# RWKV-7 recurrence: alpha and key-times-a kept in DRAM between two stages, and the head normalisation on ScalarE

## The chip, the cores and the metric

One NeuronCore of one Trainium2 chip runs the whole program. The metric is device time in microseconds, from the start to the end of one execution. A NeuronCore has a matrix engine (PE, with weight loads listed as PEld), VectorE (DVE), ScalarE (ACT), GpSimd (POOL) and SyncE (SP). In this kernel SP issues every DMA, in the order of its queue.

## The reference

The program is one inference step of a two-layer decoder trunk on 1040 prompt tokens (16 of them learned) and 8 x 8 sample tokens: a gated DeltaNet layer, then an RWKV-7 layer. The change is in the second. Cut to it:

```python
r, k, v, z = rkvz
a     = sigmoid(a0 + (xs[5] @ a1) @ a2)
kk    = l2norm((k * k_k).reshape(B, T, H, N))          # 16 heads of 64
k     = k * (1.0 + (a - 1.0) * k_a)
decay = exp(-exp(w))
b     = kk * a
def step(S, (r_t, k_t, v_t, d_t, kk_t, b_t)):
    S = S * d_t + (S @ -kk_t) (x) b_t + v_t (x) k_t
    return S, S @ r_t
y = (y - mean(y)) * rsqrt(var(y) + GN_EPS) * lnx_w + lnx_b      # per head
y = (y + sum(r * k * r_k) * v) * silu(z)
out = y @ w_o
```

## The kernel before, in words

The 1104 tokens are cut into three segments of 384, 384 and 336 columns and every segment into six chunks of 64; two heads share the 128 partitions, so there are 8 pairs of heads and 24 items (segment, pair). The recurrence is computed chunk by chunk. With D the running product of decays in a chunk, the kernel forms `alpha = kk * D` (shifted by one token), `kk * a / D`, `r * D` and `k2 / D`, and a triangular system per chunk links them.

Two stages of the RWKV layer matter here.

The **inverse stage** (`rwkv_inverse`, five batches of up to five items) runs beside the big projections. For each item it loads the running decays, `a` and `k` (`rwkv_load`), computes `kk`, `D` (`Dp`) and its inverse (`iD`) on ScalarE (`rwkv_keys`), alpha into the tile `al` (a single buffer, name `sal` in the profile) on VectorE with small fixes on GpSimd (`alpha`), and `kk * a * iD` in place in `kk` (GpSimd, then VectorE). Matmuls of `kk` against `al` give the triangular matrices, which go through DRAM (`rltd`) to be inverted; the inverses are stored to DRAM (`ttd`).

The **recurrence** (`wave`) goes through 58 waves. In a wave up to three items are each at one of their chunks; an item is in work for six waves, and a new one is begun every second wave. `rwkv_front` prepares an item: it loads the same three inputs and `r` and `v` again, computes `kk`, `Dp` and `iD` again, and builds two operands. `AR` holds alpha and `r * D`; alpha is made by GpSimd (L1280, L1281, L1283), `r * D` by VectorE (L1354). `BK` holds `k2 * iD` (VectorE, L1357 and L1361) and `kk * a * iD` (GpSimd, L1358 and L1362). Then `pr` (L1367) is made for the bonus term. Later waves take the item's parts: `scores` (matmuls of `BK` against `AR` into the PSUM tiles `fG`, masked by VectorE into `G`, L1391 and L1393), `keys` (transposes of `BK` into `fBT`, copied by ScalarE into `BT`, L1402), `values` (transposes of `v` into `fVT`, copied by ScalarE into the ring `UV`, L1415) and `bonus`. All these PSUM tiles share a ring of two buffers with the name `f`.

The chain of a wave is: `step_solve` (PE, then ScalarE's copy into `X`, L1483), `step_inner` (PE, then two ScalarE evictions into `UV`, L62), `step_state` (PE `rS` and `rY`, then VectorE's update of the state, L1525, which needs ScalarE's `pre`, and ScalarE's copy of the outputs into `y`, L1533). Between these, PE works on the output projection and the gate projection; their weights come as tiles `wraw`, split into a high half `whi` (ScalarE, L86) and a low half `wlo` (GpSimd, L90).

`rwkv_finish` normalises an item's outputs over each head. VectorE takes mean and variance (`bnst`, `mv`), GpSimd a power (`grs`, L103) which VectorE refines (L104 to L106), and GpSimd applies them chunk by chunk, six operations of 128 x 64 (L1551). In the next but one wave PE transposes `y` (`fyT`). The sample states of the first eight items are read (`rwkv_sample_read`, with matmuls against `AR`) and written (`rwkv_sample_write`) in the first 16 waves or so.

PE's instructions in the recurrence stand in the order in which the program gives them. The order on all other engines, SP's DMAs among them, and PE's outside the recurrence, is set by a scheduler that simulates the program while it is built.

Of the kernel before, what the change touches and what calls it, by code (L numbers as in the profile page):

```python
# [10 lines left out]
AF = mybir.ActivationFunctionType  # L11
ALU = mybir.AluOpType
# [23 lines left out]
class Builder:  # L36
# [8 lines left out]
    def t(self, pool, shape, tag, bufs=1, dt=F32):  # L45
        self.uid += 1
        return pool.tile(shape, dt, name=f"{tag}_{self.uid}", tag=tag, bufs=bufs)
# [1200 lines left out]
    def rwkv_open(self):  # L1248
        self.rk2 = self.t(self.cp, [128, 144], "rk2")
        self.csd, self.ad, self.rd, self.vd, self.zd, self.kd = (self.dram([8, 128, 1152], n) for n in  # L1250
                                                                 ("csd", "ad", "rd", "vd", "zd", "kd"))
        self.ttd = self.dram([24, 128, 384], "ttd")

    def rwkv_load(self, n, pool, tag, names):
        nc, t = self.nc, self.t
# [9 lines left out]
    def rwkv_keys(self, p, ld, pool, tag):  # L1265

        nc, t = self.nc, self.t
        kk = t(pool, [128, 384], tag + "kk", 2 if tag == "s" else 1)
        self.act(kk, ld["k"], AF.Identity, scale=self.pcol["rwkv_k_k"][:, p:p + 1])
        Dp, iD = t(pool, [128, 385], tag + "Dp", 1), t(pool, [128, 384], tag + "iD", 1)  # L1270
        nc.gpsimd.memset(Dp[:, 0:1], 1.0)
        self.act(Dp[:, 1:385], ld["cs"], AF.Exp, scale=-self.DEC)
        self.act(iD, ld["cs"], AF.Exp, scale=self.DEC)
        return kk, Dp, iD

    def alpha(self, al, kk, Dp, s, eng):

# [10 lines left out]
    def rwkv_inverse(self, b, pool):  # L1288

        items = range(5 * b, min(5 * b + 5, 24))  # L1290
        nth = 6 * len(items)
        nc, t = self.nc, self.t
        ltd, ssd = self.dram([nth, 128, 64], f"rltd{b}"), self.dram([nth, 128], f"rssd{b}")
        for q, n in enumerate(items):
            s, p = divmod(n, 8)
            names = ("cs", "a", "k")
            ld = self.ahead or self.rwkv_load(n, pool, "s", names)
            kk, Dp, iD = self.rwkv_keys(p, ld, pool, "s")

            self.ahead = self.rwkv_load(n + 1, pool, "s", names) if n < 23 else None  # L1300
            sq = t(pool, [128, 384], "sgl", 2)
            self.act(sq, kk, AF.Square)
            al = t(pool, [128, 6, 64], "sal", 1)
            self.alpha(al, kk, Dp, s, nc.vector)
            nc.gpsimd.tensor_tensor(kk, kk, ld["a"], op=ALU.mult)
            nc.vector.tensor_tensor(kk, kk, iD, op=ALU.mult)
            gp = self.ps("f", 2, "L")
            ssp = self.ps("f", 2, "rss")
            for c in range(6):
                for h in (0, 1):  # L1310
                    a = 64 * h
                    self.mm(gp[a:a + 64, 64 * c:64 * c + 64], kk[a:a + 64, 64 * c:64 * c + 64], al[a:a + 64, c, :])
            self.mm(ssp[0:2, 0:384], self.hmask, sq)
            gl = t(pool, [128, 6, 64], "sgl", 2)
            nc.scalar.copy(gl, gp[:, 0:384].rearrange("p (c i) -> p c i", i=64))
            if s == 0:
                nc.gpsimd.tensor_tensor(gl[:, 0, :], gl[:, 0, :], self.m_strs2, op=ALU.mult)
            nc.sync.dma_start(ltd[6 * q:6 * q + 6].rearrange("c q i -> q c i"), gl)
# [12 lines left out]


    def rwkv_front(self, p, s):

        nc, t, ap, fp, col = self.nc, self.t, self.ap, self.fp, self.pcol
        P = Ctx()
        P.p, P.s, P.n = p, s, 8 * s + p
        NB = self.NB
# [4 lines left out]
        def system():  # L1343
            nc.sync.dma_start(P.TT.rearrange("p c k -> p (c k)"), self.ttd[P.n])
        ld = self.rwkv_load(P.n, fp, "f", ("cs", "k", "a", "r", "v"))
        kk, Dp, iD = self.rwkv_keys(p, ld, fp, "f")
        DC = P.DC = t(fp, [128, 14], "DC", NB + 2)
        nc.gpsimd.tensor_copy(DC[:, 0:6].unsqueeze(2), Dp[:, 1:385].rearrange("p (c k) -> p c k", k=64)[:, :, 63:64])
        if s == 0:
            nc.gpsimd.tensor_copy(DC[:, 6:14].unsqueeze(2), Dp[:, 1:65].rearrange("p (c k) -> p c k", k=8)[:, :, 7:8])  # L1350
        AR = P.AR = t(fp, [128, 6, 2, 64], "AR", NB + 1)
        c6 = lambda x: x.rearrange("p (c k) -> p c k", k=64)
        self.alpha(AR[:, :, 0, :], kk, Dp, s, nc.gpsimd)
        nc.vector.tensor_tensor(AR[:, :, 1, :], c6(ld["r"]), c6(Dp[:, 1:385]), op=ALU.mult)  # L1354
        k2 = t(fp, [128, 384], "k2", 1)
        self.act(k2, ld["a"], AF.Identity, scale=pc("rwkv_k_a"), bias=self.omka[:, p:p + 1])
        nc.vector.tensor_tensor(k2, k2, ld["k"], op=ALU.mult)  # L1357
        nc.gpsimd.tensor_tensor(kk, kk, ld["a"], op=ALU.mult)  # L1358

        BK = t(fp, [128, 6, 2, 64], "BK", 2)  # L1360
        nc.vector.tensor_tensor(BK[:, :, 0, :], c6(k2), c6(iD), op=ALU.mult)  # L1361
        nc.gpsimd.tensor_tensor(BK[:, :, 1, :], c6(kk), c6(iD), op=ALU.mult)  # L1362
        flat = lambda x: x.rearrange("p x k -> p (x k)")
        yield P

# [14 lines left out]
        def scores(c):  # L1380

            gp = [self.ps("f", 2, "G") for h in (0, 1)]
            for u in range(3):
                for h in (0, 1):
                    q = slice(64 * h, 64 * h + 64)
                    self.mm(gp[h][:, 128 * u:128 * u + 128], flat(BK[q, c + u]), flat(AR[q, c + u]))
            for h in (0, 1):
                g3 = gp[h][:, 0:384].rearrange("p (q k) -> p q k", k=128)
                f = 0
                if s == 0 and c == 0:  # L1390
                    nc.vector.tensor_tensor(G[:, 0, h, :], g3[:, 0, :], self.gms, op=ALU.mult)  # L1391
                    f = 1
                nc.vector.tensor_tensor(G[:, c + f:c + 3, h, :], g3[:, f:3], self.gm.unsqueeze(1).broadcast_to([128, 3 - f, 128]),  # L1393
                                        op=ALU.mult)
# [67 lines left out]
    def step_solve(self, W):  # L1462

        hs = [slice(0, 64), slice(64, 128)]
        UV = self.ring_uv(W.tau)
        for (P, ci), q in zip(W.items, W.at):
            for h in (0, 1):
                self.mmw(W, "X", h, 64 * q, P.G[:, ci, h, 0:64], UV[:, q, h])
        for (P, ci), q in zip(W.items, W.at):
            if 6 * P.s + ci > 1:  # L1470
                S = self.S[P.p]
                for x, name in ((0, "X"), (1, "Y")):
                    for h in (0, 1):
                        self.mmw(W, name, (h + x) % 2, 64 * q, P.AR[hs[h], ci, x], S[hs[h]])
        nc = self.nc
        lo, hi = min(W.at), max(W.at) + 1
        P, ci = W.items[-1]
        with self.tc.high_priority():
            if P.s == 0 and ci == 0:
                hi -= 1  # L1480
                nc.vector.tensor_tensor(W.X[:, hi], W.pX[:, 64 * hi:64 * hi + 64], P.xs[:, 0], op=ALU.add)
            if lo < hi:
                nc.scalar.copy(W.X[:, lo:hi].rearrange("p c k -> p (c k)"), W.pX[:, 64 * lo:64 * hi])  # L1483
# [51 lines left out]
    def rwkv_finish(self, p, s, P):  # L1535

        nc, t, ap, col = self.nc, self.t, self.ap, self.pcol
        c0, n = SEGS[s]
        y = lambda q: self.ring_y(2 * P.n + q)[:, 2 - q // 2]
# [7 lines left out]
        va, rs = t(ap, [128, 6], "va", 2), t(ap, [128, 6], "grs", 2)  # L1547
        nc.vector.tensor_scalar(va, mv[:, :, 1], GN_EPS, None, op0=ALU.add)
        self.rsqrt(rs, va, ap, "gn")
        for q in range(6):  # L1550
            nc.gpsimd.tensor_scalar(y(q), y(q), mv[:, q, 0:1], rs[:, q:q + 1], op0=ALU.subtract, op1=ALU.mult)  # L1551
        yield
        yp = self.ps("f", 2, "yT")
        for q in range(6):
# [17 lines left out]
    def rwkv_sample_read(self, P):  # L1572
# [16 lines left out]
        for b in range(8):  # L1589
            for h in (0, 1):  # L1590
                a = 64 * h
                self.mm(rp[a:a + 64, 16 * b:16 * b + 16], P.Sb[a:a + 64, b, :], AR[a:a + 64, 0, :, 8 * b:8 * b + 8])
        q = t(ap, [128, 2, 8, 8], "rkst", 1)
        nc.vector.tensor_copy(q, rp[:, 0:128].rearrange("p (b x r) -> p x b r", b=8, x=2))
        yield
# [373 lines left out]
```

## Time and profile before

| | us |
|---|---|
| median of 3 runs | 2374.34 |
| lowest and highest | 2370.59, 2375.54 |
| the profiled execution's own time | 2374.91 |
| its span | 2373.2 |
| inverse stage beside the projections | about 1465 to 1845 |
| recurrence | about 1845 to the end |

| engine | busy us | share of the span |
|---|---|---|
| PE | 2168.7 | 91% |
| VectorE | 1617.0 | 68% |
| ScalarE | 1248.0 | 53% |
| GpSimd | 1113.8 | 47% |

A row of the profile gives line, engine, operation, and what is written and read by the program's names; `[2.04 <-DVE G L1393]` at the end of a row of the timeline says that the engine stood idle for 2.04 us before it until VectorE's `G` of line 1393 was done. An SP row is the issue of a DMA, not its transfer. Shares are means over stages that have different limits.

### The profile page before, as it was taken

To read this page: it belongs to the slowest core of one execution; us is meant where nothing else is said; L and a number is where in the kernel's file an instruction comes from. 1 tells how busy PE (TensorE), PEld (TensorE's weight loads), DVE (VectorE), ACT (ScalarE), POOL (GpSimd) and SP (SyncE) were. 2 spreads that over 40 slices of the span, in tenths; PEclk is the share of its full clock that TensorE was granted. 3 is DMA by queue.
4 is the path that set the end of the run, shared out by engine and by line. 5 is a ranking of instruction groups with operands and counts; after the bars stand their busy time and mean duration, and the time that the engine had idled before them with its cause. 6 is when DMAs were issued, how large, how long until landed. Compare 5 with 4: busy or idle time off the path is not lost. (4 is left out here: it accounts for less than half of the span.)

```text
span 2373.2 us, 54463 instructions
## 1 busy us (share of the span) xinstructions
PE 2168.7 (91%) x19737; PEld 1962.9 (83%) x19737; DVE 1617.0 (68%) x4195; ACT 1248.0 (53%) x3479; POOL 1113.8 (47%) x1566
## 2 busy tenths in 40 slices
PE   5989999999999999999989998998999888888886
PEld 5888989888898989898989998987878776777775
DVE  6868677685858686873346724389896666778754
ACT  5455655554656555566243646555453454556552
POOL 3435343343444353433223513355454666777764
PEclk9999999999999999999999999999999999999998
DMA  3323332324233333435262245566754544555543
GB/s 113 106 74 104 87 102 78 96 71 113 68 105 94 85 98 88 115 107 163 62 165 76 72 156 173 143 164 165 188 135 129 178 115 141 158 178 182 178 138 125
DMA packets 470535, 290.01 MB, mean 122 GB/s; under 512 B 188121, under 2 KB 455642, under 8 KB 470266
## 3 DMA queue, kind: packets, MB, share of 16 engines
q1 hardware_dynamic: 470266, 286.53, 42.7%
q8 instruction: 156, 2.56, 0.5%
q14 instruction: 113, 0.93, 0.1%
HBM read 200.53 MB, written 85.89 MB: 121 GB/s over the span
## 5 line engine op out<-in xcount | busy, mean ns | idle before, releaser
L90 POOL TENSOR_TENSOR wlo<-wraw,whi 128x512 fp32r<-128x512 f32 (+2 forms) x252 | 329.7, 1311 | 349.2 <-ACT whi L86 323.2
L76 PE MATMUL d<-xc,whi 128*128 128x384 f32 (+2 forms) x910 | 259.1, 341 | 4.8 <-POOL xc L90 2.8
L86 ACT CAST whi<-wraw 128x512 fp32r<-128x512 f32 (+2 forms) x252 | 151.6, 603 | 130.6 <-PE dq L76 50.5
L419 DVE SCALAR_TENSOR_TENSOR cvy<-raw,cw,cvy 128x408 f32<-128x408 f32 (+2 forms) x288 | 178.9, 634 | 17.6 <-ACT cvy L62 15.7
L452 DVE TENSOR_TENSOR invtmp<-invA,invT 72x31 f32<-72x31 f32 (+31 forms) x403 | 170.4, 423 | 13.0 <-DMA invA<-ltd 5.1
L76 PEld LDWEIGHTS d<-xc,whi 128*128 128x128 f32 (+1 forms) x910 | 167.8, 191 | 12.6 <-issue 5.3
L454 DVE TENSOR_TENSOR invT<-invT,invtmp 72x31 f32<-72x31 f32 (+31 forms) x403 | 168.9, 419 | 6.7
L76 PE MATMUL dz<-xc,whi 128*128 128x384 f32 (+1 forms) x480 | 148.3, 340 | 0.0
L76 PE MATMUL dv<-xc,whi 128*128 128x384 f32 (+1 forms) x480 | 146.8, 335 | 0.0
L76 PE MATMUL d<-xc,wlo 128*128 128x384 f32 (+2 forms) x428 | 142.7, 342 | 0.0
L76 PE MATMUL d<-xa,whi 128*128 128x384 f32 (+3 forms) x450 | 139.0, 344 | 3.3 <-DVE xa L90 1.7
L868 POOL TENSOR_SCALAR Sb<-Sb,eglb 128x128 f32<-128x128 f32 x128 | 81.3, 651 | 88.1 <-DMA Sb<-in_state_gdn 23.7
L1551 POOL TENSOR_SCALAR y<-y,mv,grs 128x64 f32<-128x64 f32 x144 | 83.8, 599 | 42.8 <-DVE grs L106 40.0
L76 PE MATMUL dv<-xa,whi 128*128 128x384 f32 (+1 forms) x288 | 99.9, 347 | 0.1
L76 PE MATMUL dz<-xa,whi 128*128 128x384 f32 (+1 forms) x288 | 99.5, 346 | 0.0
L76 PEld LDWEIGHTS d<-xa,whi 128*128 128x128 f32 (+1 forms) x450 | 84.3, 192 | 9.7 <-issue 3.3
L76 PEld LDWEIGHTS dz<-xc,whi 128*128 128x128 f32 x480 | 88.9, 191 | 0.8
L76 PEld LDWEIGHTS dv<-xc,whi 128*128 128x128 f32 x480 | 88.5, 188 | 0.5 <-issue 0.4
L76 PE MATMUL d<-xh,wlo 128*128 128x384 f32 (+1 forms) x256 | 85.2, 348 | 1.6 <-POOL wlo L90 1.6
L76 PE MATMUL d<-xa,wlo 128*128 128x384 f32 (+3 forms) x252 | 86.4, 343 | 0.0
L76 PE MATMUL d<-xh,whi 128*128 128x384 f32 (+1 forms) x256 | 84.5, 344 | 0.5 <-ACT whi L86 0.5
L76 PE MATMUL d<-xl,whi 128*128 128x384 f32 (+1 forms) x256 | 84.5, 347 | 0.0
(514 smaller groups left out, 7171.7 us busy)
## 6 DMA issues: line engine op xcount, KB each, us to landing
wraw<-in_gdn_w_in SPq DMA_DIRECT2D x96, 256.0 KB
wraw<-in_rwkv_w_rkvz SPq DMA_DIRECT2D x80, 256.0 KB
Sb<-in_state_gdn SPq DMA_DIRECT2D x64, 256.0 KB
wraw<-in_rwkv_w_o SPq DMA_DIRECT2D x40, 256.0 KB
E<-drow SPq DMA_DIRECT2D x24, 384.0 KB
attn<-drow SPq DMA_DIRECT2D x24, 384.0 KB
wraw<-in_gdn_w_out SPq DMA_DIRECT2D x36, 256.0 KB
out_s_gdn<-Sb SPq DMA_DIRECT2D x32, 256.0 KB
```

Source lines behind the costliest of these rows:

```text
L76: self.nc.tensor.matmul(out, lhsT, rhs, start=start, stop=stop)
L86: nc.scalar.copy(hi, x)
L90: e.tensor_tensor(lo, x, hi.bitcast(F32), op=ALU.subtract)
L419: nc.vector.scalar_tensor_tensor(y[:, 0:wd], raw[:, k:k + wd], cw[k], y[:, 0:wd], op0=ALU.mult, op1=ALU.add)
L452: nc.vector.tensor_tensor(tmp, A[:, j, j + 1:32].unsqueeze(2).broadcast_to([nb, n, m]), Tv[:, j, 0:m].unsqueeze(1).broadcast_to([nb, n, m] ...
L454: nc.vector.tensor_tensor(Tv[:, j + 1:32, 0:m], Tv[:, j + 1:32, 0:m], tmp, op=ALU.subtract)
L868: nc.gpsimd.tensor_scalar(Sb[:, u], Sb[:, u], self.eglb[:, hv, 4 * g + u:4 * g + u + 1], None, op0=ALU.mult)
L1551: nc.gpsimd.tensor_scalar(y(q), y(q), mv[:, q, 0:1], rs[:, q:q + 1], op0=ALU.subtract, op1=ALU.mult)
```

## The change

Three things are done.

1. The inverse stage stores `al` and `kk * a * iD` of each item to two new DRAM arrays (`ald`, `bkd`): 48 DMAs of 192 KB.
2. The front of the recurrence no longer computes `kk`, alpha and `kk * a * iD`. It loads them: 24 DMAs into `AR` and 24 into every second block of 64 columns of `BK`. `AR` changes its layout from `[6, 2, 64]` to `[2, 6, 64]`, and its readers follow. `rwkv_keys` is split, so that the front calls only the decay part.
3. `y` is normalised on ScalarE as `rs * y + nm`, where `nm = -mean * rs` (tile `gnm`) is one more small VectorE operation, instead of `(y - mean) * rs` on GpSimd.

```diff
-        self.ttd = self.dram([24, 128, 384], "ttd")
+        self.ttd, self.ald, self.bkd = (self.dram([24, 128, 384], n) for n in ("ttd", "ald", "bkd"))
...
     def rwkv_keys(self, p, ld, pool, tag):
-        kk = t(pool, [128, 384], tag + "kk", 2 if tag == "s" else 1)
+        kk = t(pool, [128, 384], tag + "kk", 2)
         self.act(kk, ld["k"], AF.Identity, scale=self.pcol["rwkv_k_k"][:, p:p + 1])
+        return kk, *self.rwkv_decays(ld, pool, tag)
+
+    def rwkv_decays(self, ld, pool, tag):
         Dp, iD = t(pool, [128, 385], tag + "Dp", 1), t(pool, [128, 384], tag + "iD", 1)
...
-        return kk, Dp, iD
+        return Dp, iD
...
             nc.gpsimd.tensor_tensor(kk, kk, ld["a"], op=ALU.mult)
             nc.vector.tensor_tensor(kk, kk, iD, op=ALU.mult)
+            nc.sync.dma_start(self.ald[n], al.rearrange("p c k -> p (c k)"))
+            nc.sync.dma_start(self.bkd[n], kk)
...
-        kk, Dp, iD = self.rwkv_keys(p, ld, fp, "f")
+        Dp, iD = self.rwkv_decays(ld, fp, "f")
...
-        AR = P.AR = t(fp, [128, 6, 2, 64], "AR", NB + 1)
+        AR = P.AR = t(fp, [128, 2, 6, 64], "AR", NB + 1)
+        BK = t(fp, [128, 6, 2, 64], "BK", 2)
+        nc.sync.dma_start(AR[:, 0].rearrange("p c k -> p (c k)"), self.ald[P.n])
+        nc.sync.dma_start(BK[:, :, 1, :], self.bkd[P.n].rearrange("p (c k) -> p c k", k=64))
         c6 = lambda x: x.rearrange("p (c k) -> p c k", k=64)
-        self.alpha(AR[:, :, 0, :], kk, Dp, s, nc.gpsimd)
-        nc.vector.tensor_tensor(AR[:, :, 1, :], c6(ld["r"]), c6(Dp[:, 1:385]), op=ALU.mult)
+        nc.vector.tensor_tensor(AR[:, 1], c6(ld["r"]), c6(Dp[:, 1:385]), op=ALU.mult)
...
-        nc.gpsimd.tensor_tensor(kk, kk, ld["a"], op=ALU.mult)
-
-        BK = t(fp, [128, 6, 2, 64], "BK", 2)
+
         nc.vector.tensor_tensor(BK[:, :, 0, :], c6(k2), c6(iD), op=ALU.mult)
-        nc.gpsimd.tensor_tensor(BK[:, :, 1, :], c6(kk), c6(iD), op=ALU.mult)
...
-                    self.mm(gp[h][:, 128 * u:128 * u + 128], flat(BK[q, c + u]), flat(AR[q, c + u]))
+                    self.mm(gp[h][:, 128 * u:128 * u + 128], flat(BK[q, c + u]), AR[q, :, c + u])
...
+        nm = t(ap, [128, 6], "gnm", 2)
+        nc.vector.scalar_tensor_tensor(nm, mv[:, :, 0], -1.0, rs, op0=ALU.mult, op1=ALU.mult)
         for q in range(6):
-            nc.gpsimd.tensor_scalar(y(q), y(q), mv[:, q, 0:1], rs[:, q:q + 1], op0=ALU.subtract, op1=ALU.mult)
+            self.act(y(q), y(q), AF.Identity, scale=rs[:, q:q + 1], bias=nm[:, q:q + 1])
```

More of the change, by code (lines that the diff above doesn't have):

```diff
@@ L1267, in rwkv_keys @@
         nc, t = self.nc, self.t
-        kk = t(pool, [128, 384], tag + "kk", 2 if tag == "s" else 1)
+        kk = t(pool, [128, 384], tag + "kk", 2)
         self.act(kk, ld["k"], AF.Identity, scale=self.pcol["rwkv_k_k"][:, p:p + 1])
+        return kk, *self.rwkv_decays(ld, pool, tag)
+    def rwkv_decays(self, ld, pool, tag):
+        nc, t = self.nc, self.t
         Dp, iD = t(pool, [128, 385], tag + "Dp", 1), t(pool, [128, 384], tag + "iD", 1)
@@ L1473, in step_solve @@
                     for h in (0, 1):
-                        self.mmw(W, name, (h + x) % 2, 64 * q, P.AR[hs[h], ci, x], S[hs[h]])
+                        self.mmw(W, name, (h + x) % 2, 64 * q, P.AR[hs[h], x, ci], S[hs[h]])
         nc = self.nc
@@ L1591, in rwkv_sample_read @@
                 a = 64 * h
-                self.mm(rp[a:a + 64, 16 * b:16 * b + 16], P.Sb[a:a + 64, b, :], AR[a:a + 64, 0, :, 8 * b:8 * b + 8])
+                self.mm(rp[a:a + 64, 16 * b:16 * b + 16], P.Sb[a:a + 64, b, :], AR[a:a + 64, :, 0, 8 * b:8 * b + 8])
         q = t(ap, [128, 2, 8, 8], "rkst", 1)
```

## The prediction

> **What bounds the kernel now.** I read the busy time by stretch first, then who waited for whom, then one pair of waves in order of time. The profiled execution took 2374.9 us, with a span of 2373.2 us, 0.6 us over the median of the runs (2374.3); every sum below is made against 2374.9.
>
> ```profile
> span 2373.2 us, 54463 instructions
> ...
> core 0: us, PE busy (x) PEld busy (x) DVE busy (x) ACT busy (x) POOL busy (x), PEclk, DMA share, GB/s
> 1465.00:1845.00 380.00, 349.93 (x3276) 310.28 (x3276) 285.80 (x583) 197.40 (x425) 183.62 (x253) 0.93 0.60 156
> 1845.00:2020.00 175.00, 145.60 (x1883) 121.81 (x1881) 112.81 (x304) 86.11 (x226) 120.20 (x169) 0.92 0.49 141
> 2020.00:2290.00 270.00, 237.12 (x3559) 199.94 (x3559) 206.15 (x568) 154.22 (x431) 202.40 (x260) 0.96 0.56 171
> ```
>
> The change lies in four stretches: the inverse stage (1465 to 1845), and the recurrence, which has a first part with the sample states (to 2020), a steady part (to 2290) and a tail. PE has the most work in all of them; what counts is therefore PE's idle time, in the steady part 270.0 - 237.1 = 32.9 us. The next lines are PE's waits, one of the steady part, one of the first part and one of the inverse stage, each as total, times, longest.
>
> ```profile
> PE fBT L73 <- DVE G L1393: 25.1, 14, 2.1
> ...
> PE fG L76 <- ACT UV L1415: 5.8, 7, 1.4
> ...
> PE fL L76 <- DVE skk L1306: 11.1, 5, 4.2
> ```
>
> So 25.1 of the 32.9 us are one wait: the transposes into `BT` need a PSUM buffer that VectorE frees when it reads the scores into `G`, and VectorE comes to `G` late. The steady part is PE-bound but for this. In the first part that wait hardly shows; there ScalarE's copies out of `fVT` (L1415) hold up the scores.
>
> **Part 1: four GpSimd multiplies leave the recurrence.** Per front GpSimd loses L1280, L1358, L1362 and the small copies, per finish the six of L1551. First VectorE's four front operations over the 24 fronts (min/median/max in ns), then one wave from 2102 us, by engine.
>
> ```profile
> L1354 DVE TENSOR_TENSOR AR<-fldr,fDp x24: 548/1930/2941, 1850.8 to 2260.6; 128x384 f32<-128x384 f32 x24
> ...
> L1357 DVE TENSOR_TENSOR k<-k,fldk x24: 579/1050/1553, 1851.8 to 2262.8; 128x384 f32<-128x384 f32 x24
> L1361 DVE TENSOR_TENSOR BK<-k,fiD x24: 546/1321/1506, 1853.3 to 2264.1; 128x384 f32<-128x384 f32 x24
> L1367 DVE SCALAR_TENSOR_TENSOR pr<-fldr,pcol,k x24: 604/1346/1619, 1853.8 to 2265.4; 128x384 f32<-128x384 f32 x24
> ```
>
> ```profile
> 2102.69 2.03 DVE L1354 TENSOR_TENSOR AR<-fldr,fDp 128x384 f32<-128x384 f32 x1 [0.27 <-ACT fDp L62]
> ...
> 2105.10 1.04 DVE L1357 TENSOR_TENSOR k<-k,fldk 128x384 f32<-128x384 f32 x1
> ...
> 2106.32 1.38 DVE L1361 TENSOR_TENSOR BK<-k,fiD 128x384 f32<-128x384 f32 x1
> 2107.62 1.35 DVE L1367 SCALAR_TENSOR_TENSOR pr<-fldr,pcol,k 128x384 f32<-128x384 f32 x1
> ...
> 2109.05 0.98 DVE L1393 TENSOR_TENSOR G<-fG,gm 128x384 f32<-128x384 f32 x2
> ```
>
> ```profile
> 2102.06 1.01 POOL L90 TENSOR_TENSOR yl<-lz,yh 128x384 fp32r<-128x384 f32 x1
> 2103.03 1.27 POOL L90 TENSOR_TENSOR wlo<-wraw,whi 128x512 fp32r<-128x512 f32 x1
> ...
> 2104.73 1.00 POOL L1280 TENSOR_TENSOR AR<-fkk,fDp 128x384 f32<-128x384 f32 x1
> ...
> 2106.28 1.01 POOL L1358 TENSOR_TENSOR fkk<-fkk,flda 128x384 f32<-128x384 f32 x1
> 2107.36 1.19 POOL L1362 TENSOR_TENSOR BK<-fkk,fiD 128x384 f32<-128x384 f32 x1
> ...
> 2109.62 0.63 PE L73 MATMUL fBT<-ident,BK 128*128 128x128 f32 x3 [2.04 <-DVE G L1393]
> ```
>
> Each slow VectorE multiply ends some 0.4 us after the GpSimd operation it meets: `k` at 2106.14 (GpSimd's alpha until 2105.73), `BK` at 2107.70 (2107.29), `pr` at 2108.97 (2108.55), and `AR` at 2104.72 behind `wlo` (2104.30). The first three meet what is removed: at their fastest they give back 1.04 - 0.58, 1.38 - 0.55 and 1.35 - 0.60, together 2.04 us. `AR` meets `wlo`, which stays, so I give it nothing; bounds for it are 0 and 2.03 - 0.55 = 1.48 us. The row's 2.04 us of PE wait is thus just paid for. Over the steady part at most 25.1 us can be had. [...]
>
> **Part 2: six normalisations move from GpSimd to ScalarE.** On GpSimd nobody waited for them. In the order of the built program all six stand on ScalarE between the copy of `X` and the two evictions into `UV`, in nearly every pair, and with them `UV` (the recurrence's chain) and all of ScalarE's later work queue behind.
>
> ```profile
> L1551 POOL TENSOR_SCALAR y<-y,mv,grs 128x64 f32<-128x64 f32 x96 | 54.6, 586 | 33.8 <-DVE grs L106 31.1 <-PE fG L76 2.7
> ...
> L62 ACT ACTIVATE pre<-rS,DC 128x64 f32<-128x64 f32 x93 | 25.7, 339 | 0.8
> ...
> L62 ACT ACTIVATE k<-flda,omka,pcol 128x384 f32<-128x384 f32 x14 | 9.7, 694 | 0.0
> L62 ACT ACTIVATE fkk<-fldk,pcol 128x384 f32<-128x384 f32 x14 | 8.6, 613 | 0.0
> ...
> 2098.43 0.17 DVE L106 SCALAR_TENSOR_TENSOR grs<-gn_t,grs 128x6 f32<-128x6 f32 x1
> ...
> 2099.40 0.33 ACT L62 ACTIVATE UV<-rX 64x192 f32<-64x192 f32 x1 [1.04 <-PE rS L80]
> 2099.63 0.31 ACT L62 ACTIVATE UV<-rS 64x192 f32<-64x192 f32 x1
> 2099.97 0.83 ACT L62 ACTIVATE pre<-rS,DC 128x64 f32<-128x64 f32 x3
> 2100.70 0.50 ACT L86 CAST yh<-lz 128x384 fp32r<-128x384 f32 x1
> ...
> 2100.89 0.57 PE L80 MATMUL rS<-UV,BT 128*64 128x64 f32 x12
> ```
>
> One such ACTIVATE (64 columns, scale and bias both from columns) is not in the trace. `pre` has a scale alone: 339 ns; a bias on top costs 694 - 613 = 81; so 420 ns, an estimate. Three `pre` take 0.83 us, so neighbours overlap by (3 x 0.339 - 0.83)/2 = 0.09; six take 2.05 us and let the next start 1.96 us after the first. Bounds: 6 x 0.25 (the pitch of `pre`) = 1.5 and 6 x 0.42 = 2.5.
> They start once `grs` (2098.60) and the new `gnm` (0.17, as `grs`) are done, near 2098.87. `UV` then starts at 2100.83 instead of 2099.40, 1.43 us later. It ends at 2101.37 (2099.94 before), and PE, which wanted it at 2100.89, comes to `rS` 0.53 late. Behind, ScalarE wins back `fkk` (0.61 less the overlap, 0.52), so `fDp` and the copies L1415 are 0.91 late; PE's scores wait for L1415 (they did so already in the first part's row), so PE is 0.91 late there. That gives PE at the `BT` transposes at 2109.62 - 2.04 + 0.91 = 2108.49. VectorE: `yh` and `whi`, on which GpSimd's `yl` and `wlo` wait, are 1.43 late, but `yl` had stood 0.86 behind the six (2102.06 against 2101.20), so `wlo` and `AR` behind it end 0.57 late. Less 2.04, the first half of `G`, done at 2109.05 + 0.49, is done at 2108.07. PE no longer waits, and the pair wins 1.1 us net.
> For the steady part: 14 waits of 25.1 us go, and all 16 pairs (96 normalisations) pay 0.91: -25.1 + 14.6 = **-10.5**. Bounds: -25.1, if ScalarE's delay is hidden, and 0.
> In the first part 5 finishes pay between 0 and 0.91 each and no `G` wait is won: **+2** (0 to 4.6).
> In the tail `wlo` was ready to start at 2334.46 and stood behind the last six on GpSimd; on ScalarE these hold up `whi` by some 0.9:
>
> ```profile
> 2332.72 3.39 POOL L1551 TENSOR_SCALAR y<-y,mv,grs 128x64 f32<-128x64 f32 x6 [0.81 <-DVE grs L106]
> ...
> 2333.95 0.51 ACT L86 CAST whi<-wraw 128x384 fp32r<-128x384 f32 x1 [3.01 <-PE do L76]
> ```
>
> So (2336.11 - 2334.46) - 0.9: **-1** (0 to -1.7).
>
> **Part 3: 48 stores in the inverse stage.** `al` is one buffer. VectorE writes the next one when PE is through with it; now the store must have landed too.
>
> ```profile
> SPq L1638 <- DMA x1T<-zst: 42.6, 27, 3.3
> ```
>
> A 192 KB write took up to 3.3 us until it let a reader go, and the matmuls that read `al` also need `kk`, which is two multiplies later; I take most landings as covered by that. Where not, VectorE slips in a stage that PE bounds. SP gets 48 issues between its weight loads, two of them waiting for VectorE. I take **+3**, from the 11.1 us that PE waits for `skk` today growing by a quarter; bounds -4 (the schedule of this stage comes out in another order) and +11 (that wait doubles).
>
> **Part 4: 48 loads in the recurrence.** No engine work. They are issued a whole pair before use. `AR` has five buffers. `BK` has two, so its load waits on SP for the transposes of two fronts back, and a weight load and a store of x1T queue behind it. I price that at nothing: the weights are loaded two tiles ahead. In the first part SP has room for two issues of 0.45 us:
>
> ```profile
> 1944.34 0.45 SPq L1262 DMA_DIRECT2D fldr<-rd  x1
> 1949.09 3.21 SPq L1580 DMA_DIRECT2D sn<-in_state_rwkv  x5
> ```
>
> If that cover fails, each pair pays what one late weight tile costs, up to 3.3 us by the row above.
>
> **Clock.** The granted clock is 0.96 in the steady part; at 1.00 throughout at most 4% of 270 us could be won, 10.8. Fewer waits should win some of it: **-3** (0 to -10.8). [...]
>
> **Sum:** -10.5 + 2 - 1 + 3 - 3 = -9.5; 2374.9 - 9.5 = **2365 us**.
>
> **The rivals.** *The cover holds.* `UV` is wanted late enough and ScalarE's delay vanishes: 2374.9 - 25.1 - 3 - 1 = 2346. For it: ScalarE is only 154 of 270 us busy. Against: in the pair shown PE wants `UV` 0.95 us after its end, and the six push it by 1.43. Chance 0.13.
> *The wait only changes its engine.* If ScalarE's shift is 25.1/16 = 1.57 us per pair instead of 0.91, PE waits as long for L1415 as it did for `G`: 2375. It takes 0.66 us more, a `gnm` that comes that much later. Chance 0.16.
> *ScalarE stands before the six.* GpSimd stood 31.1 us in 15 waits, 2.1 each, for `grs`, at no cost to anyone; if ScalarE stands like that, it is 0.91 + 2.1 = 3.0 us per pair, and `UV`, the copies L1415, `fDp` and through it VectorE's front are behind it: -25.1 + 16 x 3.0 = +23, with the first part near **2400**. It decides from 1.57 us per pair on. For it: `grs` ends behind a chain over two engines, just after `X`. Against: both hang on the same matmuls, so they stay about 0.3 us apart. Chance 0.20.
> *The stores hold up the inverse stage.* The 11.1 us treble, +22, against the gain without its +3: 2374.9 - 12.5 + 22 = 2384. Chance 0.09.
> The change does what it says (the four multiplies are gone from GpSimd's program), so that rival is left out.
>
> **How the numbers follow.** Forecast 0.42, cover holds 0.13: faster by over 0.2% (4.7 us, about what a measurement of this kernel can tell from no change) 0.55. Within it: 0.16. Slower: 0.20 + 0.09 = 0.29. The forecast's own range, by its bounds, is 2352 to 2376. For 8 in 10 I go down to 2345, to the covered case, and up to 2388, past the stores' case and short of the last one's 2400; outside are some 0.06 below and 0.13 above.
>
> **What would show it.** Right: `fBT <- DVE G` under 5 us in the steady part; `k`, `BK`, `pr` near 0.6 us with `AR` still near 1.9; six ACTIVATEs of about 0.42 us between `X` and `UV`; PE's wait for L1415 up to some 10 us and a new one for `UV` of about 8. Wrong: ScalarE idle before `y` for `gnm` over 10 us in all (third rival); PE's wait for `skk` over 20 us (fourth); weight casts waiting for their DMA in the steady part (Part 4).

## The result and the profile after

The change makes the kernel a little faster: 2370.25 us median of 20 runs (2360.47 to 2376.66) against 2375.65 us of the kernel before, run beside it (20 runs, 2370.36 to 2387.40). The ratio of the times is 0.9970, 95% interval 0.9957 to 0.9982. The profiled execution took 2370.52 us, 4.4 us less than that of before.

```profile
span 2368.8 us, 54498 instructions
...
PE 2170.3 (92%) x19737; PEld 1962.9 (83%) x19737; DVE 1575.2 (66%) x4219; ACT 1281.7 (54%) x3599; POOL 952.1 (40%) x1318
```

GpSimd lost 162 us of work (1113.8 before), VectorE 42, ScalarE gained 34; PE's work is the same. To see where the time went I cut both traces at the same matmuls: the 10000th matmul of the profile, the 14000th (start of the recurrence), the 15500th (end of its first part), the 19000th (end of the steady part) and the last. First the table of windows of the kernel before, then that of the kernel after: stretch, its length, busy time of each engine, granted clock, DMA share, GB/s.

```profile
core 0: us, PE busy (x) PEld busy (x) DVE busy (x) ACT busy (x) POOL busy (x), PEclk, DMA share, GB/s
1387.10:1884.70 497.60, 458.90 (x4002) 414.93 (x4002) 331.85 (x652) 255.82 (x547) 232.50 (x326) 0.94 0.59 161
1884.70:2010.00 125.30, 104.44 (x1507) 85.51 (x1507) 80.26 (x251) 60.67 (x167) 81.40 (x103) 0.93 0.45 131
2010.00:2278.40 268.40, 235.52 (x3503) 198.33 (x3504) 209.98 (x562) 154.41 (x429) 206.50 (x266) 0.96 0.55 167
2278.40:2361.00 82.60, 67.47 (x743) 57.09 (x743) 35.73 (x123) 32.16 (x99) 45.58 (x60) 0.94 0.46 138
```

```profile
1392.80:1899.60 506.80, 461.24 (x4001) 414.87 (x4001) 327.14 (x652) 254.47 (x544) 226.12 (x312) 0.94 0.64 178
1899.60:2029.90 130.30, 107.63 (x1505) 86.99 (x1503) 77.67 (x257) 66.09 (x187) 40.05 (x48) 0.89 0.54 155
2029.90:2276.90 247.00, 225.51 (x3501) 192.27 (x3505) 174.48 (x575) 176.21 (x509) 103.78 (x110) 0.99 0.68 203
2276.90:2356.60 79.70, 66.77 (x742) 56.32 (x743) 37.62 (x128) 39.88 (x123) 32.99 (x37) 0.94 0.48 144
```

Read the second number of each row. The stretch with the inverse stage grew by 9.2 us, the first part by 5.0; the steady part shrank by 21.4 and the tail by 2.9. Together that is -10.1; by the ratio of the runs it is -7.1 (-10.2 to -4.3). The program ahead of these stretches is the same in both, and it came 5.7 us later here (1392.8 against 1387.1); in the profiles of the other kernels below it lies between 1381.6 and 1399.2, so that is scatter, and stages are compared by their lengths alone. Even so each length comes from one execution: with `y` on VectorE the profiled one took 2348.13 us, 15 less than the median of that kernel.

In the steady part two things happened. PE's idle time (length less PE busy) fell from 32.9 to 21.5 us, and the same matmuls took 225.5 instead of 235.5 us, at a granted clock of 0.99 instead of 0.96. The waits of PE there, after (total, times, longest):

```profile
PE rS L80 <- ACT UV L62: 8.2, 13, 0.9
PE fG L76 <- ACT UV L1421: 7.7, 12, 1.4
...
PE fsT L73 <- DVE G L1399: 0.9, 3, 0.3
```

The wait of `fBT` for `G` (25.1 us) is gone; a new one for `UV` and a longer one for ScalarE's copies out of `fVT` (L1421, before L1415, where 1.5 us stood) are there in its place, 15.9 us together. VectorE's four front operations after, over the 24 fronts (min/median/max in ns):

```profile
L1363 DVE TENSOR_TENSOR AR<-fldr,fDp x24: 546/558/1666, 1865.8 to 2260.5; 128x384 f32<-128x384 f32 x24
...
L1366 DVE TENSOR_TENSOR k<-k,fldk x24: 541/820/1494, 1866.3 to 2262.5; 128x384 f32<-128x384 f32 x24
...
L1368 DVE TENSOR_TENSOR BK<-k,fiD x24: 532/536/1533, 1866.9 to 2263.2; 128x384 f32<-128x384 f32 x24
...
L1373 DVE SCALAR_TENSOR_TENSOR pr<-fldr,pcol,k x24: 602/606/1642, 1868.4 to 2263.7; 128x384 f32<-128x384 f32 x24
```

`AR`, `BK` and `pr` now mostly run at their fastest; `k` does not, with a median of 0.82 us. And this is what the six normalisations do on ScalarE: first their group in the steady part (count, busy time in us, mean in ns, idle time of ScalarE before them), then one wave in order of time.

```profile
L62 ACT ACTIVATE y<-y,gnm,grs 128x64 f32<-128x64 f32 x95 | 33.4, 428 | 15.4 <-DVE gnm L1557 15.4
```

```profile
2093.53 0.32 ACT L1489 COPY X<-rX 128x192 f32<-128x192 f32 x1 [1.37 <-PE rX L80]
2094.46 2.10 ACT L62 ACTIVATE y<-y,gnm,grs 128x64 f32<-128x64 f32 x6 [0.62 <-DVE gnm L1557]
2096.58 0.33 ACT L62 ACTIVATE UV<-rX 64x192 f32<-64x192 f32 x1
...
2097.18 0.57 PE L80 MATMUL rS<-UV,BT 128*64 128x64 f32 x12 [0.73 <-ACT UV L62]
```

ScalarE stands 0.62 us for `gnm`, works 2.10 us on `y`, and only then makes `UV`, for which PE waits 0.73 us.

### The profile page after: what moved, and what is told of

It is laid out like the page before. It is cut to its first block, busy times and chain, and to the rows that moved or that the text cites. A ratio compares the mean times of both kernels' runs of the same rounds, so it can differ in the third digit from the quotient of the medians.

```text
span 2368.8 us, 54498 instructions
## 1 busy us (share of the span) xinstructions
PE 2170.3 (92%) x19737; PEld 1962.9 (83%) x19737; DVE 1575.2 (66%) x4219; ACT 1281.7 (54%) x3599; POOL 952.1 (40%) x1318
## 5 line engine op out<-in xcount | busy, mean ns | idle before, releaser
L419 DVE SCALAR_TENSOR_TENSOR cvy<-raw,cw,cvy 128x408 f32<-128x408 f32 (+2 forms) x288 | 177.2, 628 | 16.3 <-ACT cvy L62 14.6
L454 DVE TENSOR_TENSOR invT<-invT,invtmp 72x31 f32<-72x31 f32 (+31 forms) x403 | 175.2, 435 | 6.6
L76 PEld LDWEIGHTS d<-xc,wlo 128*128 128x128 f32 (+1 forms) x428 | 82.3, 194 | 4.4 <-issue 1.9
L62 ACT ACTIVATE o<-rA,gcol 128x128 f32<-128x128 f32 x128 | 46.5, 371 | 72.0 <-DVE S L779 71.6
L62 ACT ACTIVATE attn<-attn,gcol 128x128 f32<-128x128 f32 x144 | 46.5, 390 | 72.0 <-POOL attn L579 71.9
```

Source lines behind the costliest of these rows:

```text
L62: return self.nc.scalar.activation(out, in_, func, bias=bias, scale=scale, **kw)
L76: self.nc.tensor.matmul(out, lhsT, rhs, start=start, stop=stop)
L419: nc.vector.scalar_tensor_tensor(y[:, 0:wd], raw[:, k:k + wd], cw[k], y[:, 0:wd], op0=ALU.mult, op1=ALU.add)
L454: nc.vector.tensor_tensor(Tv[:, j + 1:32, 0:m], Tv[:, j + 1:32, 0:m], tmp, op=ALU.subtract)
```

## The experiments

My theory after this reading: the DRAM part alone is worth more than the whole change; the normalisations on ScalarE give part of it back, the stores another part; and the gain in the steady part is twice the forecast because PE's 2 us waits had also cost granted clock. The rivals: what unblocked VectorE was `y` leaving GpSimd, not the four multiplies; the 9 us of the inverse stage were scatter; the clock followed something else. Ratios are against the kernel before, run beside each; its median was between 2377.3 and 2380.6 us there.

**The two halves of the change.** First the DRAM part, with `y` normalised on GpSimd as before:

```diff
-            self.act(y(q), y(q), AF.Identity, scale=rs[:, q:q + 1], bias=nm[:, q:q + 1])
+            nc.gpsimd.tensor_scalar(y(q), y(q), mv[:, q, 0:1], rs[:, q:q + 1], op0=ALU.subtract, op1=ALU.mult)
```

> The kernel after, but with y normalised on GpSimd as before: the DRAM part alone. Theory (the four front multiplies that leave GpSimd are what unblocks VectorE): PE's 25.1 us for G go as in the kernel after, the waits for UV before rS (8.2 us in the steady part after) stay small because ScalarE has no six ACTIVATEs between X and UV, the inverse stage keeps its some 9 us of loss, and the time is about 2362, 8 below the kernel after; the steady part is some 28 us shorter than before. VectorE's k, BK and pr at a median under 0.85 us. Rival (y on GpSimd is what blocked VectorE, by delaying yl and wlo): AR stays at a median of about 1.9 us, waits for G stay above 12 us, and the time is at or over 2375.

Measured: 2356.47 us median, ratio 0.9894 (0.9873 to 0.9915), some 25 us faster than before, and by the two ratios 18 faster than the kernel after. Its steady part, and PE's waits in it:

```profile
2023.30:2262.00 238.70, 226.00 (x3506) 192.16 (x3509) 181.74 (x562) 144.95 (x414) 154.28 (x204) 0.99 0.71 211
```

```profile
PE rX L80 <- DMA rTT<-ttd: 6.0, 5, 3.7
...
PE fBT L73 <- DVE G L1399: 1.2, 3, 0.7
```

The steady part is 29.7 us shorter than before: 20.2 us of idle time and 9.5 us of PE's own time. The theory holds: `k`, `BK` and `pr` run at medians of 0.550, 0.544 and 0.607 us, and `AR` is still slow at 1.156 (in the wave at 2104 us it ends 0.42 us after `wlo`), but `G` is in time all the same. Of the 18 us between this kernel and the one after, the profiles put 8.3 into the steady part (238.7 against 247.0), 6.7 into the first part (123.6 against 130.3) and 6.3 into the inverse stage, where the two kernels do the same; the tail is 4.5 longer here. A wait that no trace before had shown comes up: PE for the inverses, `rTT`.

Then the other half alone, the kernel before with `y` on ScalarE (the diff above the other way round, with `gnm`):

> The kernel before, with only y moved to ScalarE, with scale and bias. Theory: VectorE's k, BK and pr still meet GpSimd's four front multiplies, so PE's wait for G stays between 15 and 25 us in the steady part, and PE's wait for UV before rS of about 8 us comes on top; AR falls towards 0.6 us if it is the six y that held wlo back into it. Time 2374 to 2384; the inverse stage as before. Rival (y leaving GpSimd is the gain): the wait for G falls under 8 us, and the time is under 2366.

Measured: 2378.60 us, ratio 1.0001 (0.9983 to 1.0020): nothing. PE's waits in its steady part:

```profile
PE fG L76 <- ACT UV L1415: 16.5, 15, 2.5
PE rS L80 <- ACT UV L62: 7.5, 13, 0.8
PE fBT L73 <- DVE G L1393: 5.7, 5, 1.3
```

In time the theory was right, in the mechanism the rival: the wait for `G` did fall, from 25.1 to 5.7 us. `AR`'s median fell from 1.930 to 1.249 us (in the wave at 2111 us it still ends 0.41 us after `wlo`, but no longer overlaps `yl` as well) and `pr`'s from 1.346 to 0.608; PE also comes later to the transposes. Which of these did how much is not shown. But 24.0 us of waits for ScalarE took its place, and PE's idle time in the steady part is 32.8 us, as before (32.9). So the wait only changes its engine, which was the prediction's second rival; it is what the ScalarE half does by itself. Behind the DRAM part there is no wait for `G` left for it to shorten, and its cost stands alone: 0.9970/0.9894, some 0.8%.

**`y` on VectorE**, the third engine that could do it, with the DRAM part:

```diff
-            self.act(y(q), y(q), AF.Identity, scale=rs[:, q:q + 1], bias=nm[:, q:q + 1])
+            nc.vector.tensor_scalar(y(q), y(q), mv[:, q, 0:1], rs[:, q:q + 1], op0=ALU.subtract, op1=ALU.mult)
```

> The kernel after, but y is normalised on VectorE (one operation for each of the six: minus mean, times 1/std), without the small product for the bias. Theory: ScalarE's evictions into UV follow X directly again, the 8.2 us that PE waits for UV before rS in the steady part fall under 3, VectorE has 206 - 23 + 96 x 0.15 = some 200 us of work in the steady part and gets to G in time: 2362 to 2366, 5 to 8 below the kernel after. Rival (VectorE is the tight engine, the six stand before its front and its copies): waits for G or pr come back to 10 us or more, and the time is 2370 or over.

Measured: 2362.99 us, ratio 0.9916 (0.9888 to 0.9945). The steady part took 238.3 us, as with `y` on GpSimd; PE's waits for `UV` before `rS` are gone, those for `G` are 3.9 us, and those for `rTT` 5.6. VectorE has the room: one of these operations took 0.31 us at the median (the 0.15 that the expectation reckons with was the author's estimate, and no run shows it), and 95 of them kept it busy for 24.4 us of the steady part.

**The stores.** The kernel before with the two stores added, which nothing loads:

```diff
+            nc.sync.dma_start(self.ald[n], al.rearrange("p c k -> p (c k)"))
+            nc.sync.dma_start(self.bkd[n], kk)
```

> The kernel before, plus the 48 stores of al and of key times a in the inverse stage; nothing loads them, and the recurrence computes them again as before. Theory (the stores hold the inverse stage up): the stage is some 9 us longer, the recurrence unchanged, time about 2383. Rival (the 9 us came from something else than the stores, as from the order of the first recurrence fronts or from the scatter of runs): 2373 to 2377.

Measured: 2384.32 us, ratio 1.0024 (1.0008 to 1.0040). The stretch with the inverse stage:

```profile
1393.20:1897.30 504.10, 458.76 (x4004) 414.23 (x4002) 329.98 (x652) 255.64 (x547) 236.25 (x326) 0.95 0.63 178
```

It is 6.5 us longer than before, the whole time 5.7 us. So the loss is the stores', and smaller than the 9.2 us of the one profile of after. To find what in them costs, one of the two arrays alone was stored, each in turn:

> The kernel before, plus the 24 stores of key times a alone (kk has two buffers); al is not stored, and nothing loads what is stored. The seven profiles so far put the inverse stage (from the 10000th matmul to the 14000th) at 497 us without stores and at 500 to 507 with all 48. Theory A (al, a single buffer, is held until its store has landed): the stage is back at 496 to 499. Theory B (every DMA more on SP's queue costs, whatever it stores): half of the loss, 499 to 501. Time by A as before, by B 2 to 3 us above it.

> The kernel before, plus the 24 stores of al alone. Theory A (al's single buffer is held): the stage takes 501 to 506 us as with all 48 stores, and the time is 4 to 7 us above before. Theory B (each DMA costs): 499 to 501, as with the other 24.

Measured: with key times a alone 2386.82 us, ratio 1.0036 (1.0018 to 1.0054), stretch 501.5 us; with alpha alone 2385.70, 1.0026 (1.0003 to 1.0049), 499.3 us. The stretches lie nearer to theory B, half the loss for half the stores, but they are one profile each, and the whole times don't show the half; in the alpha run 5.6 us of it are a longer first part (130.9 us at a clock of 0.87), in which nothing had been changed. What speaks against theory A is a wait that can be read directly: VectorE stood 1.0 us in all for a store of `al` to land with all 48 stores, and never with alpha's 24 alone. `al` with its single buffer is not the reason. The tile that is held is `kk`, in spite of its two buffers: ScalarE stood 6.0 us in 6 waits for a store of key times a to land before it could write the next `kk` with all 48 stores, and 16.0 us in 8 with those 24 alone. Whether PE pays for this is not shown; its own wait for `skk` did not grow (11.1 us before, 10.7 in both). Last, the stores behind the triangular matrices' (with three `zst` buffers, see below):

> The DRAM part alone with three zst buffers, and the two stores of an item in the inverse stage issued at the end of the item, behind the stores of its triangular matrices, on which the inversion waits. Theory (the inverse stage loses its some 6 us because the triangular matrices stand behind 384 KB on SP's queue): the stage is 3 to 6 us shorter than with the early stores, and so is the time. Rival (the loss is the scheduler's other order of the stage, whatever the place of the stores): the stage's length within 2 us of the early stores', or longer.

Measured: 2357.51 us, ratio 0.9912 (0.9893 to 0.9932), stretch 503.9 us against 502.3 with the early stores. Nothing of the 3 to 6 us came. Over all profiles the stretch took 495.9 to 497.7 us in four kernels without stores (mean 497.0), 499.3 and 501.5 with 24, and 499.7 to 507.0 with 48 (eight kernels, mean 503.4): some 6 us for 48 stores, with a scatter of the same size among the eight. Why the stores cost this stays open; `kk` with a third buffer was not tried.

**The late inverses.** In the DRAM part alone SP waited for stores of `x1T` before it could reload the tile `zst`, and the load of `rTT` was queued behind. In the steady part this came to 57.8 us in 26 waits (the 63 us in the expectations below are of a longer window, from 1990 to 2280 us):

```profile
SPq L1644 <- DMA x1T<-zst: 57.8, 26, 4.4
```

So `zst` got a third buffer, once with `y` on GpSimd and once with it on VectorE:

```diff
-                x = t(self.fin, [128, 384], "zst", 2)
+                x = t(self.fin, [128, 384], "zst", 3)
```

> The DRAM part alone (y on GpSimd), and the tile zst, through which the output projection adds to x1T, with three buffers instead of two. Theory: in the faster recurrence SP stands 63 us for the store of x1T to land before it may load the next zst, and the loads of the inverses (rTT) behind it on the queue come too late, so that PE waits 6.0 us for them. With a third buffer SP's wait for x1T falls under 25 us, PE's waits for rTT under 1 us, and the time is 4 to 7 below that of the DRAM part alone: some 2350. Rival (rTT is late for another reason, such as its place in the queue): PE still waits 4 us or more for rTT, and the time is that of the DRAM part alone, 2356.

> The kernel after with y normalised on VectorE, and zst with three buffers. Same theory as for three buffers on the DRAM part alone: 5.6 us of PE's waits for rTT go; 2354 to 2360 by the 2363 of the two-buffer version, and about the same steady part as the version with y on GpSimd, some 233 us. Rival: VectorE, with 47 us of y more, sets the pace once SP does not: PE's waits for rS of VectorE or for G grow by 4 us or more, and the time stays at 2360 or over.

Measured: with `y` on GpSimd 2358.06 us, ratio 0.9908 (0.9885 to 0.9930); on VectorE 2352.03, 0.9894 (0.9869 to 0.9918). SP's wait in the steady part of GpSimd's version:

```profile
SPq L1644 <- DMA x1T<-zst: 45.9, 19, 4.3
```

It fell by a fifth, not below 25 us as expected, and on VectorE's version not at all (57.4 before, 55.8 with three buffers): the third buffer took little of SP's wait, so that step of the theory is wrong. PE's wait for `rTT` fell all the same, to 2.3 us (0.7 on VectorE's version), and the steady part by 2.5 and 5.1 us. In the whole time the first version shows nothing of it, and the second's interval overlaps that of its two-buffer form.

**The clock.** In the kernel before, the windows of 2 us around the pair that the prediction shows, whose wait for `G` ended at 2109.62 (the granted clock is the third number from the end):

```profile
2108.00:2110.00 2.00, 0.38 (x3) 0.31 (x3) 2.00 (x5) 0.94 (x2) 0.91 (x2) 0.99 0.90 273
2110.00:2112.00 2.00, 2.00 (x27) 1.70 (x26) 0.70 (x4) 0.79 (x3) 1.88 (x2) 0.50 1.01 354
2112.00:2114.00 2.00, 2.00 (x9) 1.81 (x8) 0.99 (x7) 0.10 (x1) 1.13 (x1) 0.66 0.51 159
2114.00:2116.00 2.00, 2.00 (x63) 1.79 (x64) 1.51 (x5) 0.52 (x2) 0.21 (x1) 1.00 0.34 118
```

Just after the wait PE ran at half clock: 2 x 0.50 + 2 x 0.34 = 1.7 us lost, which is 3.4 us at 0.50. The same stands behind the waits for `G` that ended at 2021.8 (there 6.8 us at 0.50), 2058.9, 2144.0, 2215.2 and 2249.6 (1.72 to 2.13 us); seven others over 1.5 us (1.57 to 1.91), which ended at 2042.4, 2076.7, 2093.2, 2127.5, 2161.9, 2233.4 and 2267.4, have no such tail.

In these traces it goes with where a wait falls. In the trace of the kernel before the 34 stretches at half clock begin on one grid of steps of 3.413 us, to within 4 ns, and in that of the kernel after the 33 do; they last one to three steps. Two steps of this grid around the wait that ended at 2109.62, and three around the one that ended at 2127.5:

```profile
2106.55:2109.96 3.41, 1.37 (x9) 1.03 (x8) 3.41 (x6) 2.10 (x7) 2.24 (x3) 1.00 0.88 256
2109.96:2113.38 3.42, 3.42 (x31) 3.08 (x30) 1.52 (x10) 0.93 (x3) 2.43 (x3) 0.50 0.74 254
...
2123.62:2127.03 3.41, 2.02 (x22) 1.50 (x19) 3.41 (x8) 1.42 (x6) 2.67 (x5) 1.00 0.82 261
2127.03:2130.44 3.41, 2.90 (x36) 2.47 (x36) 2.55 (x13) 1.78 (x4) 2.62 (x3) 1.00 0.89 300
2130.44:2133.86 3.42, 3.42 (x86) 3.02 (x86) 2.58 (x9) 0.89 (x3) 1.78 (x3) 1.00 0.47 142
```

The first wait (2.04 us) lies in one step, and the next step is at half clock. The second (1.91 us) is split by a border into 1.39 and 0.52 us, and nothing follows. All 14 waits of this steady part come out so: behind 1.72 us or more of idle time in one step the next one is at half clock, behind 1.54 us or less it is not. Beyond this stretch the border is not as sharp: in the steady part of the kernel after the one step at half clock, from 2196.76, came behind a step with 1.40 us.

The same recurrence, unchanged, was profiled four times, in the kernel before and in the three with stores alone (48, alpha's 24, key times a's 24). Its steady part has 7, 6, 5 and 4 steps at half clock there (granted clock 0.96, 0.96, 0.97 and 0.97) and takes 268.4, 266.1, 265.3 and 263.4 us: their number changes from profile to profile, and one step, 3.413 us at 0.50, is worth 1.7 us.

To try this cause alone, PE was given useless work to fill the waits, with nothing taken from any engine: eight products of the identity with itself before the transposes, into columns that nobody reads.

```diff
         def keys(c):
-            tp = self.ps("f", 2, "BT")
+            tp, _ = self.ps("f", 2, "BT"), [self.mmx(self.W.pY[:, 256:384], self.ident, self.ident) for _ in range(8 * (c == 0 and s > 0))]
```

> The kernel before, unchanged but for useless work: ahead of the transposes of the first half of BK (where PE waits for G) of the 16 items of the second and third segment, PE multiplies the identity with itself eight times into columns of the PSUM tile of Y that nobody reads. Nothing is taken away from any engine, and VectorE is as late with G as before. Theory (the 2 us waits cost the granted clock as well: each of the longest is followed by some 3.4 us at half clock): the waits for G shrink by the 1.5 us or so of useless work each, the clock of the steady part rises from 0.96 to 0.98 or 0.99, the other matmuls take up to 10 us less, and the kernel with more work is faster: 2366 to 2374, the steady part 3 to 10 us shorter. Rival (the clock follows something else, such as heat or the mean load): clock stays at 0.96, and the time is the same or up to 6 us longer, 2376 to 2384.

Measured: 2377.16 us, ratio 0.9996 (0.9977 to 1.0015); no change in time is shown. Its steady part, with 240 more instructions on PE, is at the clock of the kernel after, and as long as the shortest of the four above:

```profile
2014.90:2278.40 263.50, 253.83 (x3741) 221.26 (x3742) 209.73 (x562) 154.69 (x429) 206.42 (x265) 0.99 0.55 170
```

Its tail is 4.7 us longer: it holds one of the useless batches and no wait for it to fill. So the work was cut to five products, in the steady part only (`5 * (c == 0 and 8 <= P.n < 23)`):

> The useless work ahead of BK's transposes again, in the kernel before, but five products instead of eight (1.87 us were eight, so some 1.2 us), and only for the 15 items whose transposes lie in the steady part, where 14 of them wait 1.8 us on average: it now fits into the wait, and the tail pays nothing. Theory (the waits cost the granted clock as well): PE stands only some 0.6 us per wait, no half-clock stretch follows, the other matmuls of the steady part take 8 to 10 us less, the stretch of 268 us is 5 to 9 us shorter with 18 us more work in it, and the time is 0.998 to 0.996 of the kernel before's. Rival (PE's total idle time sets the clock, or the clock is not worth a time): the stretch is 266 us or longer, and the ratio 0.999 to 1.002.

Measured: 2374.78 us against 2380.63, ratio 0.9981 (0.9965 to 0.9997). Its steady part:

```profile
2002.90:2266.00 263.10, 245.12 (x3656) 211.54 (x3660) 209.38 (x562) 154.69 (x430) 205.66 (x266) 0.99 0.56 171
```

Two steps at half clock are left, as with eight products, against the four to seven of the unfilled recurrence, and the clock is 0.99 against 0.96 and 0.97; VectorE, ScalarE and GpSimd are as busy as before (209.4, 154.7, 205.7 us). That PE's waits of some 2 us cost clock is thus shown. That useless work makes the kernel faster is shown only just: the interval ends at 0.9997, eight products gave nothing, and the stretch is 5.3 us shorter than in the profile of before but only 0.3 us shorter than the shortest unfilled one.

**A version with `y` on two engines.** `y` on GpSimd for the eight items of the first segment and on VectorE for the others, with the DRAM part and three `zst` buffers:

```diff
-            self.act(y(q), y(q), AF.Identity, scale=rs[:, q:q + 1], bias=nm[:, q:q + 1])
+            (nc.vector if s else nc.gpsimd).tensor_scalar(y(q), y(q), mv[:, q, 0:1], rs[:, q:q + 1], op0=ALU.subtract, op1=ALU.mult)
```

> The DRAM part with three zst buffers, and y normalised by GpSimd for the eight items of the first segment and by VectorE for the other sixteen. Theory (each engine where it was the cheaper: the first part took 124 us with y on GpSimd and 129 to 134 with it on VectorE; the steady part and the tail 311 us with it on VectorE and 322 on GpSimd): 2342 to 2348. Rival (the two placements don't add up, since the first part's shorter time lets SP's or VectorE's queue run late in the steady part): 2352 to 2358, as for the unmixed versions.

Measured: 2346.67 us (2345.08 to 2350.10, 5 runs) against 2380.20, ratio 0.9866 (0.9844 to 0.9887): some 32 us faster than before. Its interval overlaps those of the DRAM part alone and of `y` on VectorE with three buffers (both 0.9894), so that mixing the two placements is better than either is not shown. Its recurrence:

```profile
1894.90:2022.30 127.40, 106.95 (x1505) 86.66 (x1501) 77.57 (x250) 57.45 (x161) 57.45 (x75) 0.91 0.55 158
2022.30:2258.10 235.80, 225.07 (x3502) 192.33 (x3506) 192.23 (x634) 145.09 (x414) 112.73 (x133) 0.99 0.72 215
2258.10:2335.90 77.80, 65.79 (x742) 55.50 (x743) 43.89 (x147) 32.22 (x99) 32.41 (x36) 0.96 0.46 141
```

## Why the prediction was right, and where its terms were off

The forecast was 2365 us by a sum of -9.5; the runs gave 2370.25, and -7.1 by their ratio. The direction, the range and the mechanism came out; two terms were mis-sized in opposite directions. (The range 2352 to 2376 that it gives "by its bounds" doesn't follow from them: the lower bounds of the five terms together give 2333.3, the upper ones 2390.5.)

*Steady part, -10.5 without the clock: right.* PE's idle time fell by 11.4 us. The 25.1 us went, and ScalarE's delay came back as 8.2 us for `UV` (about 8 was named) and 7.7 for L1421 (up to some 10), of which 1.5 had stood there before: 14.4 more, against 14.6. Within this, `k` gave back less than was worked out (median 0.82 us, not 0.58) and `AR` more (below). The price of one normalisation, 0.42 us, measured 0.428, and six took 2.10 us against 2.05. One sign against the forecast did show: ScalarE stood 15.4 us for `gnm` in all, more than the 10 us named, so the third rival's mechanism was at work. It came to 1.0 us per pair, neither the 0.3 that the forecast reckoned with nor the rival's 2.1, and PE's price stayed at 15.9/16 = 1.0 us per pair, below the 1.57 from which that rival decides.

*`AR` keeps its 1.9 us: wrong, with little effect on the sum.* Its median fell to 0.558. The wave shown above, first GpSimd and then VectorE:

```profile
2098.46 1.01 POOL L90 TENSOR_TENSOR yl<-lz,yh 128x384 fp32r<-128x384 f32 x1 [5.24 <-ACT yh L86]
2099.42 1.63 POOL L90 TENSOR_TENSOR wlo<-wraw,whi 128x512 fp32r<-128x512 f32 x1
```

```profile
2099.36 0.56 DVE L1363 TENSOR_TENSOR AR<-fldr,fDp 128x384 f32<-128x384 f32 x1 [0.81 <-ACT fDp L62]
2100.65 0.82 DVE L1366 TENSOR_TENSOR k<-k,fldk 128x384 f32<-128x384 f32 x1
```

`AR` now starts 0.11 us before `yl` ends and gets through before `wlo`, which takes 1.63 us instead of 1.27; `wlo` is met by `k` instead, which ends 0.42 us after it (2101.47 against 2101.05) and is still 0.82 long. I had kept the old order of `AR` and `wlo`. As PE had no wait for `G` left to lose, nothing more came of it. (`AR` runs at 0.56 us although `wlo` is on record beside it, and `wlo` is 0.36 us longer than in the wave of before. Whether one stands while the other works is not shown.)

*Clock, -3: too small.* The matmuls of the steady part took 10.0 us less, near the end of the bounds (-10.8), and the statement that at most 25.1 us could be had there is wrong for that reason: with `y` on GpSimd the stretch lost 29.7. The time at half clock fell from seven steps of the grid to one, which is worth 10.2 us. The profile of before has the most such steps of the four, so this is its high end: from four steps it would be 5.1. The step that failed is the one that took the loss of clock as a share of the whole stretch, instead of looking at where it fell: right behind the waits that the change removes. The -3 itself has no row behind it; what the trace of before shows is half clock, 1.7 us lost in a step, behind each of the six waits that left PE idle for 1.72 to 2.13 us in one step of the grid.

*Inverse stage, +3: too small.* It is 6.4 by the means of the profiles, 5.7 by the runs with the stores alone (1.9 to 9.5), and 9.2 in the one profile of after. The fourth rival's mechanism did not happen, nor the one that the term was made of: PE's wait for `skk` went from 11.1 to 9.9 us. VectorE's next `al` waited 0.9 us in all for a store to land, and ScalarE's next `kk`, which the forecast did not look at, 5.9 us. (The 3.3 us that the prediction takes for a write are the longest time that SP stood for one.) PE's idle time in the stretch grew from 38.7 to 45.3 us with the stores alone (length less PE busy), spread over 34 waits where there had been 23.

*First part, +2: 5.0 in the profile.* PE's idle time there grew by 1.8 us and its own matmuls by 3.2, at a granted clock of 0.89 against 0.93. That lies within noise of the same size: the clock was 0.87 (130.9 us) in a kernel in which the recurrence had not been touched. Behind the DRAM part this stretch took 123.6 to 127.4 us in the four kernels with `y` on GpSimd there and 129.2 to 134.4 in the three with it on ScalarE or VectorE, so leaving GpSimd may cost something here; whether it does stays open. *Tail, -1: -2.9*, the direction right.

*Loads, 0: right for this change*, where PE never waits for them in the steady part. But the cover is thin: in the kernel whose steady part is another 8 us shorter, PE waits 6.0 us for `rTT` on the same queue.

So the answer to where the expected gain went: the steady part won 21.4 us against the one profile of before, 18.8 against the mean of the four with the same recurrence (265.8), where 13.5 were forecast with the clock; 6 to 9 us of it were paid in the inverse stage for the data, and some 8 us (247.0 against 238.7) were never won there because ScalarE, on the chain of the recurrence, got work that GpSimd or VectorE could do beside it.

## What to carry to other kernels

Before moving work off a loaded engine, ask which engine stands on the chain of the loop: the same six operations made the steady part 8 us longer on ScalarE, the engine with the most room, than on GpSimd or VectorE (247.0, 238.7 and 238.3). Price two halves of a change separately: here one was worth 25 us, the other nothing alone and a loss on top. And when PE waits about 2 us again and again, look at the granted clock in windows of 2 us behind those waits: removing one is worth its length, and some 1.7 us more where half clock followed it. Profile an unchanged stretch more than once before reading a difference of 5 us from it: here it took 263.4 to 268.4 us in four kernels.

## What the runs showed of the hardware that was not expected

In the trace of the kernel before and in that of the kernel after, the stretches at half clock begin on one grid of steps of 3.413 us (34 and 33 of them, to within 4 ns). In the kernel before, a step of the steady part in which PE stood idle for 1.72 to 2.13 us was followed by one at a granted clock of 0.50; waits of up to 1.91 us that a border of the grid split into parts of at most 1.54 were not. One such step costs about 1.7 us, so the same recurrence took 263.4 to 268.4 us with four to seven of them. Filling the waits with useless matmuls (five products each time) left two such steps and raised the clock of the stretch from 0.96 to 0.99, at a ratio of the times of 0.9981 (0.9965 to 0.9997). The 48 stores of 192 KB made a stretch that PE bounds longer by 6.4 us (means of eight profiles with and four without), though PE itself waits for none of them.
